# Rotary tables made in the first dilated pair, and HGRN2's level products held for both heads' updated queries

## The chip, the cores and the metric

The kernel runs on one core of a Trainium2 chip. A core has five engines that run side by side, each with its own queue of instructions in a fixed order: TensorE (PE, matrix products, results in PSUM banks), VectorE (DVE), ScalarE (ACT), GpSimd (POOL) and SyncE (SP), which here issues the DMA transfers. The metric is the device time of one execution in microseconds (us), the median of several runs. The time before is 1779.11 us, the median of three runs from 1778.2 to 1780.48.

## The reference

The function is a two-layer encoder on one sequence of 512 tokens with 1024 channels. Each layer makes one combined projection of its input and feeds three token mixers from it. Their outputs are gated, projected, merged, projected once more and normalized.

```python
def _layer(x, pos, ...):
    p = _split_in(jnp.einsum('bsd,dn->bsn', x, w_in) + b_in)
    y_a = _rms_norm(_hgrn2(p['hg_q'], p['hg_f_fwd'], p['hg_f_bwd'], p['hg_i'], lb_f, lb_b), hg_norm)
    y_a = y_a * jax.nn.silu(p['hg_g'])
    y_b = _dilated_mixer(groups) * jax.nn.silu(p['dil_g'])
    y_c = _mla(p['mla_cq'], p['mla_ckv'], p['mla_kr'], pos, g_q, g_kv, w_uq, w_ukv)
    y_c = y_c * jax.nn.silu(p['mla_g'])
    branch = jnp.einsum('nbsc,ncd->nbsd', jnp.stack([y_a, y_b, y_c]), w_branch)
    merged = jnp.sum(jax.nn.sigmoid(p['merge']) * branch, axis=0)
    return _layer_norm(ALPHA * x + jnp.einsum('bsd,de->bse', merged, w_out), ln_g, ln_b)
```

- A, HGRN2: a gated linear recurrence with eight heads, forward and backward in time: `S_t = diag(f_t) S_{t-1} + k_t v_t^T`, `o_t = S_t^T q_t`.
- B, dilated attention: eight heads in three groups of windows, with a linear bias by distance, a softmax in each group and a weighted sum over the groups.
- C, latent attention (MLA) with four heads. Part of its queries and keys is turned by a rotary embedding:

```python
ang = pos[..., None] * inv            # inv = theta ** (-i / half)
cos, sin = jnp.cos(ang), jnp.sin(ang)
x1 * cos - x2 * sin,  x2 * cos + x1 * sin
```

## The kernel before, in words

Activations lie with channels on the 128 partitions and the 512 tokens along the free dimension; a projection of 128 channels is one PSUM bank of 128x512. Every large product is made in three passes, since each operand is split into a high and a low part: high by high, low by high, high by low. With 1024 input channels that makes 24 matmuls of 128x512 per bank (`mm3`, L300; `tm` does the same with tokens on the partitions, L317). Weights come in chunks of 128x1024: SP loads a chunk into one of two raw buffers (L280), ACT copies the high part (L274), and POOL subtracts it from the raw chunk for the low part (L275; DVE for the chunks of HGRN2).

PSUM has four banks for projections, three for smaller products (`at_bank`) and one for outputs. Tiles in SBUF come from rotating pools by tag: `a2` has 16 buffers, `acc` 8, `f2` 8, `a4` 4, `f4` 6. A tile that takes a buffer waits for the last reader of the one before.

**The order.** The code is written as a sequence of calls, but a scheduler fixes the order on each engine when the kernel is built. It plans with its own estimates of how long each instruction takes, from the dependencies, the buffers and the order in the code. An edit that moves a call, or that adds a dependency, so changes the order of other work too. `after(first, *before)` adds such a dependency by hand: the instruction `first` waits for all of `before`.

**HGRN2.** The heads are worked on in four pairs. `hgrn_gates` makes for a head the query tile and the gate tiles `fr` (forget) and `kk` (keys) from three projections (hq, and hf twice). `in_tm(C_HI, "hv")` makes the values, whose banks DVE empties (L514). `hgrn_levels` is a generator that builds a head's 64-token block products by doubling the distance m = 1, 2, 4 ... 64. At each level the query tile `qq` and the key tile `kk` are multiplied in place by products of gates (L771 and L772, on DVE), so that the level's products (L754, on PE, tile `hs`) see the decayed queries and keys; ACT copies the keys into `kc` (L742) first. The products of level 4 are a case of their own (L723); the products of the higher levels are handed to the caller with `yield [made], products`, where `made` is the copy into `kc`. The caller runs the two heads of a pair in step, issues both heads' products one behind the other, and ties the first of them to both heads' `made`. Between these small groups PE runs the projections of the next pair. `hgrn_out` normalizes the outputs: a sum of squares (hgms, L534), the inverse root by small DVE instructions on 128x4 (hgrs), its spread over the partitions by a product (hgrb, L544), then the multiplications on DVE (L857, L858) and the split (L252).

**Dilated attention.** For each of four head pairs `dil_scores` makes the scores in four groups of small matmuls, two for the first window group (dsa, L924) and two for the others (dsb, L948). DVE adds the bias and takes the row minimum of the negated scores in the same instruction (`biased_min`, L895; tiles za and zb, minima in dst). The minima of both kinds go through DRAM to the other layout (L971 to L983) and come back as dso; DVE joins them (L990), ACT makes the exponentials (L996 for za, L1001 for zb), and later PE multiplies them with the values. Behind the first pair's exponentials in the code stands `merge(0, 0, ya)`, which begins the branch projection: PE's br products on the weights wb_0.

**Rotary tables.** `rope_tables` (L322) makes cos and sin of position times frequency once, in layer 0. It loads the positions (L327), reduces the angle to -pi..pi in exact steps by 43 DVE instructions on 128x512 (L329 to L378), and ACT takes two Sines (L376, L379) and makes four copies or scalings (L380 to L382). They are first read in `mla_rope`, behind all dilated pairs (at 642 us in the trace of before).

## Time and profile before

| | |
|---|---|
| median of three runs | 1779.11 us |
| profiled execution, its own time | 1780.54 us |
| its span | 1778.8 us |
| mean granted TensorE clock | 0.995 |
| busy: PE, DVE, ACT, POOL | 1745.7, 1048.8, 731.7, 574.6 us |

The span is the time from the first to the last instruction that the profiler saw; the profiled execution's own time lies 1.74 us above it. In a row of the timeline stand the start and the length in us, the engine, the line, the operation, output <- inputs with their kind, the count, and in brackets the idle time ahead of it with what ended it. Rows of the waits give the total, the number and the longest in us. Rows of groups give the busy time in us and the mean of one instruction in ns, and rows of windows give each engine's busy time in the order PE, weight loads, DVE, ACT, POOL, then the granted clock, the DMA share and GB/s.

### The profile page before, as it was taken

The numbers are of one execution on the slowest core, as the hardware profiler recorded it, in microseconds if no ns is written. First come the engines' busy times: TensorE is split into PE (matmuls) and PEld (weight loads), VectorE is DVE, ScalarE is ACT, GpSimd is POOL, SyncE is SP. The second block draws the span as 40 slices with busy tenths as digits, with TensorE's granted clock in tenths as the row PEclk, the third lists the DMA queues.
The fourth block names the chain that finished last, engine by engine and source line by source line (L and its number), as shares of the span: only waits on it lengthen the run. The fifth ranks groups of instructions, "written<-read, shape, count | busy, mean of one in ns | idle before, by whom it ended". The sixth has DMA issues, their size and how long they took to land.

```text
span 1778.8 us, 26441 instructions
## 1 busy us (share of the span) xinstructions
PE 1745.7 (98%) x10616; PEld 1451.2 (82%) x10616; DVE 1048.8 (59%) x1886; ACT 731.7 (41%) x1273; POOL 574.6 (32%) x338
## 2 busy tenths in 40 slices
PE   9999999999999999999999999999999999999987
PEld 7778978988888888887788888888888888888876
DVE  8888777443232566656577778775333225656566
ACT  6445453242424354433254355442424244434330
POOL 0412244233333243333213122532434332333341
PEclk9999999999999999999999999999999999999999
DMA  5223222223323222422242222222323222324222
GB/s 193 83 66 102 75 73 85 79 65 95 84 72 91 62 79 74 144 81 70 95 137 89 85 78 73 88 82 74 78 66 106 72 84 46 98 74 149 76 71 71
DMA packets 77146, 154.15 MB, mean 87 GB/s; under 512 B 37728, under 2 KB 37856, under 8 KB 77024
## 3 DMA queue, kind: packets, MB, share of 16 engines
q1 hardware_dynamic: 77024, 152.47, 28.0%
q8 instruction: 83, 1.36, 0.3%
q14 instruction: 39, 0.32, 0.1%
HBM read 148.15 MB, written 4.29 MB: 86 GB/s over the span
## 4 chain that ended last, share of the span: by engine, by line
PE 61%; DVE 4%; ACT 2%; DMA 1%; issue 1%; POOL 1%; SPq 0%; DVEq 0%; ACTq 0%
PE mg L300 14%; PE dl L300 6%; PE br L300 5%; PE wo L1236 5%; PE hf L300 4%; PE dv L317 4%; PE cq L300 2%; PE hq L300 2%; PE mo L659 2%; PE ckv L300 1%; PE hgg L300 1%; PE hv L317 1%; PE do L1016 1%; PE st L498 1%; PE qn L300 1%; PE dg L300 1%
## 5 line engine op out<-in xcount | busy, mean ns | idle before, releaser
L772 DVE TENSOR_TENSOR kk<-kk,fr 128x512 f32<-128x512 f32 x96 | 93.4, 992 | 32.8 <-ACT kc L742 21.7
L693 POOL TENSOR_TENSOR qq<-hq,fr 128x1024 f32<-128x1024 f32 x16 | 42.5, 2655 | 199.3 <-DVE fr L686 179.5
L771 DVE TENSOR_TENSOR qq<-qq,fr 128x512 f32<-128x512 f32 x96 | 75.3, 797 | 17.0 <-POOL qq L693 15.2
L1076 DVE TENSOR_SCALAR mg<-mg 128x512 f32<-128x512 f32 x32 | 53.4, 1680 | 54.0 <-ACT mg L1075 53.9
L895 DVE CUSTOM_DVE_ANT_0 zb<-dsb,con 128x256 f32<-128x256 f32 x64 | 23.3, 421 | 46.4 <-PE dsb L948 46.3
L764 DVE COPY_PREDICATED ha<-mask,hs 64x256 f32<-64x256 uint8 (+1 forms) x80 | 40.4, 505 | 16.7 <-PE hs L754 15.5
L655 ACT COPY mpt<-mtr 128x128 f32<-128x128 f32 x64 | 17.1, 266 | 77.7 <-DVE mpt L655 77.7
L275 POOL TENSOR_TENSOR wb_1l<-wb_1r,wb_1h 128x1024 fp32r<-128x1024 f32 x12 | 29.4, 2449 | 58.9 <-ACT wb_1h L274 45.0
L275 POOL TENSOR_TENSOR wb_0l<-wb_0r,wb_0h 128x1024 fp32r<-128x1024 f32 x12 | 29.4, 2448 | 58.8 <-ACT wb_0h L274 44.9
L878 DVE TENSOR_SCALAR dl<-dl,par,con 128x512 f32<-128x512 f32 x24 | 25.8, 1076 | 38.0 <-PE dl L300 37.9
L754 PEld LDWEIGHTS hs<-qq,kc 128*64 128x64 f32 x1024 | 33.3, 137 | 17.6 <-issue 8.8
L732 POOL TENSOR_SCALAR_AFFINE_SELECT ha<-hc 128x256 f32<-128x256 f32 x32 | 12.8, 424 | 105.0 <-ACT hc L727 104.8
L754 PE MATMUL hs<-qq,kc 128*64 128x64 f32 x1024 | 38.2, 225 | 5.6 <-DVE qq L771 5.6
L996 ACT ACTIVATE za<-za,dst 128x256 f32<-128x256 f32 x64 | 30.0, 471 | 33.4 <-DVE dst L990 33.4
L655 DVE COPY mpt<-mtr 128x128 f32<-128x128 f32 x64 | 18.5, 289 | 39.6 <-PE mtr L653 31.6
L713 POOL TENSOR_TENSOR hk<-kk,f 128x256 f32<-128x256 f32 x32 | 23.8, 745 | 51.5 <-DVE fr L775 51.5
L789 ACT COPY hkt<-hkt 128x384 f32<-128x384 f32 x32 | 15.4, 480 | 60.3 <-PE hkt L787 59.9
L1076 DVE TENSOR_SCALAR mgc<-mgc 128x512 f32<-128x512 f32 x16 | 24.8, 1547 | 25.0 <-ACT mgc L1075 25.0
L742 ACT COPY kc<-kk 128x512 f32<-128x512 f32 x64 | 37.6, 621 | 4.2 <-DVE kk L772 4.1
L650 DVE TENSOR_SCALAR mp<-mp,mst 128x512 f32<-128x512 f32 x32 | 35.6, 1112 | 0.9
L1201 DVE SCALAR_TENSOR_TENSOR res<-res,wo 128x256 f32<-128x256 f32 x32 | 12.1, 416 | 38.1 <-PE wo L1236 38.0
L659 PE MATMUL mo<-mpt,mv 128*128 128x128 f32 (+1 forms) x192 | 33.5, 309 | 0.0
(1509 smaller groups left out, 5408.5 us busy)
## 6 DMA issues: line engine op xcount, KB each, us to landing
wb_0r<-in_blocks_dram SPq DMA_DIRECT2D x12, 512.0 KB, 3.6
wb_1r<-in_blocks_dram SPq DMA_DIRECT2D x12, 512.0 KB, 3.6
w_0r<-in_blocks_dram SPq DMA_DIRECT2D x9, 512.0 KB, 3.6
w_1r<-in_blocks_dram SPq DMA_DIRECT2D x8, 512.0 KB, 3.6
w_2r<-in_blocks_dram SPq DMA_DIRECT2D x8, 512.0 KB, 3.5
w_3r<-in_blocks_dram SPq DMA_DIRECT2D x8, 512.0 KB, 3.6
wo_0r<-in_blocks_dram SPq DMA_DIRECT2D x8, 512.0 KB, 3.5
wo_1r<-in_blocks_dram SPq DMA_DIRECT2D x8, 512.0 KB, 3.5
```

Of the source, the lines that this page charges most:

```text
L275: (eng or nc.gpsimd).tensor_tensor(lo, raw, hi.bitcast(F32), ALU.subtract)
L300: newest["product"] = nc.tensor.matmul(ps, lhs(a, k), rhs(b, k), start=n == 0, stop=n == 3 * kt - 1)
L317: nc.tensor.matmul(ps, xs[a][2 * j + k][:, toks], w[b][:, k], start=j == 0 and n == 0, stop=j == 3 and n == 5)
L659: nc.tensor.matmul(o[:, cols], v[:, kb, h * 128:h * 128 + 128], pts[kb][:, cols], start=qt == 1 and kb == 0, stop=qt == NT - 1 and kb == N ...
L693: nc.gpsimd.tensor_tensor(qq, bcast(q, [[0, 2], [1, S]]), fr, ALU.mult)
L742: made = A.copy(fap(kc, 0, [[2 * m, R // 2], [m, 2], [1, m]]), fap(kk, 0, [[2 * m, R // 2], [S + m, 2], [1, m]]))
L754: mat = nc.tensor.matmul(sc[rows, to], kc[:, at], rhs, start=True, stop=True)
L764: ready = [V.copy_predicated(fap(a[rows], cols.start, [[128, NT], [1, wd]]), bcast(mk, [[0, NT], [1, wd]]), fap(sc[rows], cols.start, [[12 ...
L771: V.tensor_tensor(fap(qq, 0, dims), fap(qq, 0, dims), qf, ALU.mult)
L772: V.tensor_tensor(fap(kk, 0, dims), fap(kk, 0, dims), kf, ALU.mult)
L1076: V.tensor_scalar(g, g, 0.5, 0.5, ALU.mult, ALU.add)
L1236: nc.tensor.matmul(ps, ms[a][2 * kp + k][:, tt * 128:tt * 128 + 128], wo[4 * half + kp][b][k][:, cols], start=(kp, a, b, k) == (0, 0, 0, 0 ...
```

## The change

Two edits. The first moves `rope_tables()` from behind the values of HGRN2, at the start of layer 0, to behind the exponentials of the first dilated pair in layer 0, and lets its eight temporary tiles take buffers of the pool `acc` in place of `a2`. The second lets `hgrn_levels` hand out its last query update `turned` beside `made`, so that the first product of a level group waits for the query updates of both heads. No arithmetic is added or removed; one ACT table load falls away (7 to 6).

```diff
-        pos_i = t2("pos_i", I32)
+        pos_i = t2("pos_i", I32, "acc")
-        ang, n_, r, u, w = t2("r_ang"), t2("r_n"), t2("r_r"), t2("r_u"), t2("r_w")
+        ang, n_, r, u, w = [t2(f"r_{i}", tag="acc") for i in "anruw"]
...
-            t = t2(f"r_t{e}")
+            t = t2(f"r_t{e}", tag="acc")
...
-                    yield [made], products
+                    yield [made, turned], products
...
-                V.tensor_tensor(fap(qq, 0, dims), fap(qq, 0, dims), qf, ALU.mult)
+                turned = V.tensor_tensor(fap(qq, 0, dims), fap(qq, 0, dims), qf, ALU.mult)
...
         hv = in_tm(C_HI, "hv")
-        if l == 0:
-            shared["rope"] = rope_tables()
-        cosT, sinT, krT = shared["rope"]
...
             exps = dil_exp(hp, scores, behind)
+            if hp == 0:
+                if l == 0:
+                    shared["rope"] = rope_tables()
+                cosT, sinT, krT = shared["rope"]
```

How the order moves, at three places. First PE in the third head pair of layer 0, where `hs_16` and `hs_32` are the level products of two heads (query tiles 1889 and 1892 before, 1829 and 1832 now) and hq, hf and hgg are projections; before:

```order
L300 MATMUL hq_2314<-xh,w_896l 128x512 x2
L754 MATMUL hs_16_0_2023<-qq_0_1889,kc_16_0_2024 64x64 x8
L754 MATMUL hs_16_0_2026<-qq_0_1892,kc_16_0_2027 64x64 x8
L300 MATMUL hq_2314<-xh,w_896l 128x512 x6
L300 MATMUL hf_2350<-xh,w_1920h 128x512 x8
L300 MATMUL hf_2350<-xl,w_1920h 128x512 x8
L300 MATMUL hf_2350<-xh,w_1920l 128x512 x3
L754 MATMUL hs_32_0_2055<-qq_0_1889,kc_32_0_2056 64x64 x8
L754 MATMUL hs_32_0_2058<-qq_0_1892,kc_32_0_2059 64x64 x8
```

and the same place now:

```order
L300 MATMUL hq_2254<-xh,w_896l 128x512 x8
L754 MATMUL hs_16_0_1963<-qq_0_1829,kc_16_0_1964 64x64 x8
L754 MATMUL hs_16_0_1966<-qq_0_1832,kc_16_0_1967 64x64 x8
L300 MATMUL hf_2290<-xh,w_1920h 128x512 x8
L300 MATMUL hf_2290<-xl,w_1920h 128x512 x8
L300 MATMUL hf_2290<-xh,w_1920l 128x512 x8
L300 MATMUL hf_2325<-xh,w_2944h 128x512 x7
L754 MATMUL hs_32_0_1995<-qq_0_1829,kc_32_0_1996 64x64 x8
L754 MATMUL hs_32_0_1998<-qq_0_1832,kc_32_0_1999 64x64 x8
```

The group of level 16 stands six matmuls later, and 31 instead of 25 large matmuls (25 with the two pieces of hq and hf, 6 + 8 + 8 + 3) stand between it and that of level 32.

Second DVE at the first dilated pair of layer 0, now, from the first group of the dsb minima to the last one (`zb_0_3221` and `zb_0_3222` are the two heads' scores, the tiles named r belong to the rotary tables; before, one `dl` eviction, L878, stood between these two groups):

```order
L895 ISA zb_0_3222,dst_0_3217<-dsb_0_3252,con 128x256
L895 ISA dst_0_3217 128x1
L335 TENSOR_SCALAR r_w<-r_u 128x512
L336 TENSOR_SCALAR r_n<-r_n 128x512
L336 TENSOR_SCALAR r_w<-r_w 128x512
L371 SCALAR_TENSOR_TENSOR r_r<-r_n,r_r 128x512
L340 TENSOR_TENSOR r_u<-r_u,r_w 128x512
L878 TENSOR_SCALAR dl_0_3414<-dl_3421,par_161,con 128x128x4
L371 SCALAR_TENSOR_TENSOR r_r<-r_n,r_r 128x512 x2
L372 SCALAR_TENSOR_TENSOR r_r<-r_u,r_r 128x512
L895 ISA zb_0_3221,dst_0_3217<-dsb_0_3265,con 128x256
L895 ISA dst_0_3217 128x1
```

Eight rotary instructions stand here between two groups of minima; nine more stand ahead of the first dsb group, three ahead of the second dsa group and one within the last group. Seventeen stand ahead of L857, among the hgrs instructions.

Third ACT at the first dilated pair, now (w_10560h and wb_0h are high parts of weight chunks, `dl_0_3414` is the key half of the third window group):

```order
L274 CAST w_10432h<-w_10432r 128x1024
L274 CAST w_10560h<-w_10560r 128x1024
L376 ACT_TABLE_LOAD
L376 ACTIVATE sin<-r_r 128x512
L876 ACTIVATE dl_0_3414<-dl_3453,par_161 128x128x4
L381 ACTIVATE krt<-sin 32x512
L382 COPY krt<-sin 32x512
L379 ACTIVATE cos<-r_u 128x512
L380 COPY krt<-cos 64x512
L996 ACT_TABLE_LOAD
L996 ACTIVATE za_0_3219,dden_0_3515<-za_0_3219,dst_0_3217 128x256 x3
L996 ACTIVATE za_0_3219,dden_0_3515<-za_0_3219,dst_0_3217 128x128
```

Before, the table load of the exponentials followed w_10432h at once, and w_10560h, wb_0h, a gate activation and w_4352h followed the last exponential in this order; now wb_0h and w_4352h follow it, and the gate activation stands among the exponentials. On PE, 172 large matmuls stand between hgrb and the first br product where 214 stood: the projections of the dilated pair have moved ahead of hgrb, and behind the first br product of each of its two banks fifteen matmuls of the next `dl` projection are put in.

## The prediction

> **What bounds the kernel now.** I read the page's first part, then TensorE's waits, then the timeline of the places where the change works.
>
> ```profile
> PE 1745.7 (98%) x10616; PEld 1451.2 (82%) x10616; DVE 1048.8 (59%) x1886; ACT 731.7 (41%) x1273; POOL 574.6 (32%) x338
> ```
>
> ```profile
> PE hs L754 <- DVE qq L771: 5.6, 7, 1.0
> PE hq L300 <- DVE hv L514: 3.2, 1, 3.2
> ```
>
> TensorE (PE) sets the time, so an edit counts only by what PE waits for afterwards. The change touches both of these rows: the level products (L754) wait seven times, 5.6 us in all, for the query update of VectorE (DVE, L771), and one gate projection waits 3.2 us for a PSUM bank that DVE has yet to empty (L514). All in all only 33 us of the span are not PE's, and what the change does can be as large as any one of its waits. The timeline of PE shows these waits in the first head pair of layer 0, where DVE also makes the rotary tables, and the same stretch of layer 1, where no tables are made:
>
> ```profile
> 40.06 0.62 PE L317 MATMUL hv<-w_0h,xh 128*128 128x512 f32 x2
> ...
> 66.22 2.64 PE L300 MATMUL hq<-xh,w_256h 128*128 128x512 f32 x8 [3.16 <-DVE hv L514]
> 68.66 3.06 PE L300 MATMUL hq<-xl,w_256h 128*128 128x512 f32 x8
> 71.56 1.98 PE L300 MATMUL hq<-xh,w_256l 128*128 128x512 f32 x8
> ...
> 94.30 0.69 PE L754 MATMUL hs<-qq,kc 128*64 128x64 f32 x16 [0.77 <-DVE qq L771]
> ...
> 102.94 0.69 PE L754 MATMUL hs<-qq,kc 128*64 128x64 f32 x16 [0.66 <-DVE qq L771]
> 104.57 0.69 PE L754 MATMUL hs<-qq,kc 128*64 128x64 f32 x16 [0.95 <-DVE qq L771]
> ...
> 137.18 1.10 PE L723 MATMUL hs<-hq,hk 128*64 128x64 f32 x32
> ...
> 927.84 0.62 PE L317 MATMUL hv<-w_0h,xh 128*128 128x512 f32 x2
> ...
> 1017.29 1.10 PE L723 MATMUL hs<-hq,hk 128*64 128x64 f32 x32
> ```
>
> ```profile
> 50.00:75.00 25.00, 21.84 (x117) 17.69 (x116) 23.76 (x39) 7.34 (x11) 13.35 (x12) 0.93 0.27 85
> ```
>
> The last row is the stretch from 50 to 75 us: DVE (third value) is busy for 23.76 of 25 us and PE's granted clock, third from the end, is 0.93. The clock is low because of the wait: the sixteen matmuls behind it take 5.34 us (66.22 to 71.56); at the usual pace, 8 matmuls in 1.82 us or 0.2275 each, they take 3.64.
>
> **Term 1: the tables leave the first pair.** From the first product of hv to the second pair's first products layer 0 takes 97.12 us and layer 1 takes 89.45. The 7.67 us between them are the bank wait (3.16), the slow matmuls behind it (1.7), three level waits (2.38) and 0.4 of small gaps. With the tables gone nothing else distinguishes the two stretches, so I take **-7.65**. It needs nothing of the second edit, and the largest part, wait and clock, ends as soon as DVE empties hv's banks 3.2 us earlier; about half of the tables' work, estimated below, is enough for that.
>
> **Term 2: the hold on the level products.** The edit adds a dependency to the first product of a level: the query updates of both heads instead of none but those that the matmuls read. No work is added. The first head's products are held with the second's, so filler matmuls stand in front of the whole group where half of it used to run.
>
> ```profile
> 230.08 1.15 PE L754 MATMUL hs<-qq,kc 128*64 128x64 f32 x32
> ...
> 238.73 0.69 PE L754 MATMUL hs<-qq,kc 128*64 128x64 f32 x16 [0.96 <-DVE qq L771]
> ...
> 300.26 0.69 PE L754 MATMUL hs<-qq,kc 128*64 128x64 f32 x16 [0.59 <-DVE qq L771]
> ```
>
> Outside the first pair of layer 0 four waits are left: these two (third and fourth pair), and 5.6 - 2.38 - 0.96 - 0.59 = 1.67 for their two in layer 1. In the fourth pair the changed order puts 28 matmuls (6.4 us) ahead of the waiting group, where 22 stood (5.0); 1.4 us more is enough to cover both of its waits, 0.59 and about 0.7: **-1.3**. In the third pair 31 stand there instead of 25: 7.05 us, while the second head's update was done about 7.4 us after the group before (231.2 to 238.6). A wait of 0.3 remains in the good case, but a hold of DVE as in term 3, which costs some 2.0 us, would make it 2.3 for the whole group. Bounds for that pair in both layers together: -1.9 to +2.7. I take 0, near the middle. What queues behind a held group on PE are gate projections, which have spare DVE and ACT time; they are not priced.
>
> **Term 3: the tables in their new place.** 43 DVE instructions move; two of their rows give the prices of the two kinds:
>
> ```profile
> L340 DVE TENSOR_TENSOR r_t<-r_t,r_w 128x512 f32<-128x512 f32 x4 | 2.7, 685 | 0.0
> L336 DVE TENSOR_SCALAR r_w<-r_w 128x512 f32<-128x512 f32 x5 | 2.1, 418 | 0.0
> ```
>
> 25 with one input at 0.42 and 18 with two at 0.69 are 22.9 us. Now they stand in DVE's queue around the first dilated pair. Seventeen (8.8 us) lie ahead of the multiplication by the RMS factor (L857), among the small instructions that make the factor, in a stretch where DVE is mostly idle. From there to the last score minimum lie three (1.25 us), nine (5.1), eight (4.7) and one (0.4): 11.5 us in four places, each ahead of a pair of minima (L895). The rest follow the last minimum. What has these minima behind it is seen in PE's timeline, and in those of DVE, GpSimd (POOL), ScalarE (ACT) and the DMA queue:
>
> ```profile
> 351.15 1.05 PE L544 MATMUL hgrb<-con,hgrs0y 128*128 128x128 f32 x8
> ...
> 353.20 1.66 PE L300 MATMUL dl<-xh,w_4224h 128*128 128x512 f32 x6
> ...
> 373.44 1.16 PE L948 MATMUL dsb<-dl 64*128 64x128 f32 x16
> 374.53 0.50 PE L300 MATMUL dl<-xh,w_6272h 128*128 128x512 f32 x1
> ...
> 405.72 0.39 PE L300 MATMUL br<-ya00h,wb_0h 128*128 128x512 f32 x1
> ```
>
> ```profile
> 352.24 2.72 DVE L857 SCALAR_TENSOR_TENSOR hoc<-hoc,par,hgrb 128x512 f32<-128x512 f32 x4 [3.34 <-PE hgrb L544]
> ...
> 358.67 2.89 DVE L252 TENSOR_TENSOR ya00l<-hoc,ya00h 128x512 fp32r<-128x512 f32 x1
> ...
> 365.77 2.47 DVE L524 SCALAR_TENSOR_TENSOR dg0s<-dg0s,dg0z 128x512 f32<-128x512 f32 x1
> ...
> 371.96 1.22 DVE L878 TENSOR_SCALAR dl<-dl,par,con 128x512 f32<-128x512 f32 x1 [2.17 <-PE dl L300]
> 374.63 0.42 DVE L895 CUSTOM_DVE_ANT_0 zb<-dsb,con 128x256 f32<-128x256 f32 x1 [1.45 <-PE dsb L948]
> ...
> 376.01 0.08 DVE L895 DVE_READ_ACCUMULATOR2_ANT dst<- 128x1 f32 x1
> ...
> 385.42 1.33 DVE L990 TENSOR_TENSOR dst<-dst,dso 128x8 f32<-128x8 f32 x2
> ```
>
> ```profile
> 358.62 2.39 POOL L275 TENSOR_TENSOR w_6272l<-w_6272r,w_6272h 128x1024 fp32r<-128x1024 f32 x1 [5.25 <-PE dl L300]
> 365.30 2.39 POOL L275 TENSOR_TENSOR w_7296l<-w_7296r,w_7296h 128x1024 fp32r<-128x1024 f32 x1 [4.29 <-PE dl L300]
> ```
>
> ```profile
> 386.71 0.51 ACT L996 ACTIVATE za<-za,dst 128x256 f32<-128x256 f32 x1 [1.97 <-DVE dst L990]
> ...
> 393.91 1.15 ACT L876 ACTIVATE dl<-dl,par 128x512 f32<-128x512 f32 x1
> ...
> 395.23 0.19 ACT L1001 ACTIVATION_READ_ACCUMULATOR zb<-zb,dst 128x1 f32 x1
> ...
> 396.26 1.05 ACT L274 CAST wb_0h<-wb_0r 128x1024 fp32r<-128x1024 f32 x1
> ```
>
> ```profile
> 453.90 0.38 SPq L971 DMA_DIRECT2D db<-dst  x1
> ```
>
> ```profile
> 461.56 0.27 DVE L990 TENSOR_TENSOR dst<-dst,dso 128x8 f32<-128x8 f32 x2 [7.69 <-DMA dso<-db]
> ```
>
> The chain: minima, a round trip of the row minima through DRAM, the exponentials on ACT, and behind them on ACT's queue the cast of wb_0h, which the first branch product (L300, br) needs. I time it from hgrb's start, 351.15.
>
> - Last minimum, before: 376.09, so 24.9. DVE was idle for 2.17 + 1.45 = 3.6 in it, which the moved work fills. 24.9 + 11.5 + 0.4 (a dl eviction of 1.2 moves in, one of 0.8 moves out) - 3.6 = 33.2.
> - Holds: two of the rows above take 2.89 and 2.47 us instead of about 0.68. Each starts just after a weight split began on POOL and ends with it, so a hold costs about 2.0. Two of the four splits between 351 and 375 held DVE in this way. A split comes per 24 matmuls (5.46 us): about six in 33 us, and the share of DVE's work that goes from SBUF to SBUF rises. I take two more holds, +4.0: 37.2. Bounds: none more, and four more (+8.0).
> - Round trip, 453.90 to 461.56 where DVE is free: 7.7, and 0.3 for the issue: 8.0.
> - From L990 to the first exponential 1.3 (385.42 to 386.71).
> - Exponentials from 386.71 to 395.42, less 1.0 for L876, which now lies ahead: 7.7; a gate activation now among them 0.7; the cast 1.05.
>
> Sum 55.9 us after hgrb. PE gets to br with fewer matmuls between: 172 instead of 214, 39.1 us, and the small groups, 2.05 for hgrb and the first dsa (351.15 to 353.20), about 1.0 for the second, 1.09 for each dsb: 5.2. So PE is there at 44.3, where it used to be at 54.6 with the cast done at 397.31, 8.4 us early. PE waits **+11.6** between hgrb and br, at the dsb groups and at br together; bounds +7.6 and +15.6.
>
> [...]
>
> **Small terms.** Behind wb_0h comes the cast for the next dl chunk, 1.05, and only two br matmuls (0.45) stand before the matmul that needs it: **+0.6**. A wait of some 6 us at br is longer than the 3.16 that cost 1.7 of slow clock: **+1.5**, bounds 0 (the wait is cut up) and 1.7. At no cost: both Sine activations, their table load and the copies, hidden in the round trip of 8.0 (without that cover they would add their five to six us, estimated from the 1.2 us that L876 takes and six such steps, to the exponentials); the position DMA, which is issued well before DVE's cast of it; the eight tiles that change their tag, as the accumulators of that pool are first used behind br.
>
> **Sum:** -7.65 - 1.3 + 11.6 + 0.6 + 1.5 = +4.75. Against the profiled 1780.54 (1778.8 of span and 1.7 around it) that is 1785.3. The profiled execution lies 1.4 over the median of the three runs, so against 1779.11 it is 1783.9; I say **1784**. The rivals' times are against the median too.
>
> **Rivals.**
>
> *No change (about 1779).* The tables cause no further hold. Then 7.6 instead of 11.6 is waited, and with 1.0 for the clock the sum is +0.25: 1779.4. For it: in the same rows two of four splits held nothing. Against it: the denser queue.
>
> *Faster (about 1774).* One mechanism: POOL's splits are released by PE (its row: `<-PE dl L300`), and a PE that waits at the dsb groups shifts them to where DVE reads minima out of PSUM, which shows no stretching (0.42 at L895). If neither the two old holds nor new ones fall on DVE, 7.6 becomes 3.6, and the clock stays up: -7.65 - 1.3 + 3.6 + 0.6 = -4.75, 1774.4. It decides from a wait of 4.8 downward. Against it: 11.5 us of DVE work in a row of about 34 can hardly dodge six splits of 2.4.
>
> *Heavier (about 1791).* Every split that starts in these 33 us holds DVE, where two of four did before: 15.6, the third pair's +2.7, 1.7 for the clock: -7.65 - 1.3 + 2.7 + 15.6 + 0.6 + 1.7 = +11.65, 1790.8. [...]
>
> *The hold doesn't do what it says.* It is a dependency, and PE may still stop in front of a level group for as long as before; then -1.3 is lost: +6.05, 1785.2.
>
> **How the numbers follow.** Chances: forecast 0.54, no change 0.27, faster 0.08, heavier 0.06, hold without effect 0.05. The forecast's own range goes from one hold more and no slow clock (+1.25, 1780.4) to three more, 1.7 for the clock and half of the third pair's +2.7 (+8.3, 1787.4). To hold 8 in 10 the range has to take in most of the no-change case: 1776.5 to 1789.5. A measurement of this kernel can tell about 0.2% (3.6 us) from no change: below 1775.6 is faster, above 1782.7 slower. Of the forecast about seven tenths, 0.39, lie above 1782.7, with the heavier case and the hold without effect 0.50; the rest of the forecast and the no-change case, 0.42, lie within; 0.08 below.
>
> **What would show it.** Term 1: no wait of hq for hv, clock 1.00 from 50 to 75 us, and 89 to 90 us from hv to the second pair. Term 2: L754's waits fall to two or so, in the third pair. Term 3: waits of PE at dsb for DVE's minima and one of about 6 us of br for the cast of wb_0h at L274, slow matmuls behind it, rope instructions of 2 us and more. I am wrong if br waits less than 3 us, or if the first pair of layer 0 keeps a wait that the tables did not cause.

## The result, and the profile after

The changed kernel takes 1791.39 us, the median of five runs (1788.32 to 1792.12), against 1780.4 for the kernel before (five runs, 1778.2 to 1782.11). The ratio is 1.0054, with a 95% interval from 1.0043 to 1.0066: slower by 11 us. The profiled execution took 1791.39 us as well, with a span of 1789.7 us and a granted clock of 0.994; its span is 10.9 us longer than that of before. The forecast had the sign and less than half of the size, and its range ends 1.9 us below the measured time.

TensorE's waits after, with the total, the number and the longest in us:

```profile
PE br L300 <- ACT wb_0h L274: 5.9, 2, 3.7
...
PE dsb L948 <- DVE dst L895: 4.0, 2, 2.2
PE hs L754 <- DVE qq L771: 3.2, 2, 1.6
...
PE br L300 <- POOL wb_0l L275: 1.9, 1, 1.9
```

The bank wait of hq for hv is gone, and the level waits (L754) are two instead of seven. In their place stand waits of br and of dsb, 11.8 us together (5.9, 4.0 and 1.9), and there are more of them than were forecast: br waits twice for wb_0h, and once for its low part. The row of windows from 50 to 75 us shows the first head pair without the tables, VectorE (third value) at 16.36 us instead of 23.76 and the granted clock at 1.00:

```profile
50.00:75.00 25.00, 25.00 (x164) 20.44 (x163) 16.36 (x24) 9.09 (x14) 5.33 (x10) 1.00 0.35 107
```

TensorE's timeline gives the ends of that pair, and then the first dilated pair of layer 0:

```profile
40.25 0.61 PE L317 MATMUL hv<-w_0h,xh 128*128 128x512 f32 x2
...
129.66 1.10 PE L723 MATMUL hs<-hq,hk 128*64 128x64 f32 x32
...
352.77 1.12 PE L544 MATMUL hgrb<-con,hgrs0y 128*128 128x128 f32 x8
...
371.81 1.16 PE L948 MATMUL dsb<-dl 64*128 64x128 f32 x16 [1.79 <-DVE dst L895]
...
381.06 2.08 PE L948 MATMUL dsb<-dl 64*128 64x128 f32 x16 [2.19 <-DVE dst L895]
...
407.31 0.73 PE L300 MATMUL br<-ya00h,wb_0h 128*128 128x512 f32 x2 [3.68 <-ACT wb_0h L274]
408.84 3.78 PE L300 MATMUL dl<-xh,w_4352h 128*128 128x512 f32 x8 [0.80 <-ACT mg L1075]
...
415.21 0.40 PE L300 MATMUL br<-ya00h,wb_0l 128*128 128x512 f32 x1
```

From hv to the second pair's first products it is 89.41 us (40.25 to 129.66), where it was 97.12. The first dilated pair waits four times, 8.46 us in all. Behind br the fifteen matmuls of `dl` take 6.4 us (408.84 to 415.21) where 15 at 0.2275 take 3.4: the clock is at half speed, granted 0.50 in each window of 1 us from 409 to 414. The next TensorE rows are from the second dilated pair, where nothing was forecast:

```profile
497.63 0.50 PE L300 MATMUL br<-ya00h,wb_0h 128*128 128x512 f32 x1 [2.20 <-ACT wb_0h L274]
500.06 0.63 PE L300 MATMUL br<-ya00h,wb_0l 128*128 128x512 f32 x1 [1.93 <-POOL wb_0l L275]
...
507.00 1.25 PE L1027 MATMUL dta<-con,za 128*128 128x128 f32 x10
```

The account, in us, along points that both traces have. The first transposes of the exponentials (dta, L1027) end a dilated pair here; up to those of the first pair the changed order does fifteen `dl` matmuls more (3.4 us). They are subtracted in that row and added in the next, where they are missing.

| stretch of the span | measured, after less before | forecast |
|---|---|---|
| start to hv | +0.2 | 0 |
| first head pair | -7.7 | -7.65 |
| from there to dta of the first dilated pair (411.16 before, 420.21 after) | +13.2 | +13.7, less 0.65 of term 2 |
| second dilated pair, dta to dta (to 495.06 before, 507.00 after) | +6.3 | 0 |
| all that follows, layer 1 with it | -1.1 | -0.65 |
| sum | +10.9 | +4.75 |

The miss is nearly all in one row: the second dilated pair.

What happened there stands in SP's queue, which issues the transfers. The row sums of the exponentials (dden) go through DRAM to the other layout as the minima do: two writes into the buffer dd (L981), two reads back (L982, L983). The timeline of SP's queue after, then the DMA view of the stretch from 473 to 492 us:

```profile
473.38 0.37 SPq L981 DMA_DIRECT2D dd<-dden  x1
473.85 0.45 SPq L280 DMA_DIRECT2D w_11072r<-in_blocks_dram  x1
475.25 0.36 SPq L981 DMA_DIRECT2D dd<-dden  x1
491.94 0.33 SPq L982 DMA_DIRECT2D dso<-dd  x1
...
492.88 0.36 SPq L280 DMA_DIRECT2D wb_0r<-in_blocks_dram  x1
```

```profile
DMA packets 1201, 0.54 MB, mean 29 GB/s; under 512 B 1072, under 2 KB 1072, under 8 KB 1200
...
w_11072r<-in_blocks_dram SPq DMA_DIRECT2D x1, 512.0 KB, 12.4
```

And the same queue before:

```profile
463.76 2.23 SPq L981 DMA_DIRECT2D dd<-dden  x2
474.37 0.33 SPq L982 DMA_DIRECT2D dso<-dd  x1
...
475.29 0.37 SPq L280 DMA_DIRECT2D w_11072r<-in_blocks_dram  x1
476.13 0.36 SPq L280 DMA_DIRECT2D wb_0r<-in_blocks_dram  x1
```

Before, the two writes go out together and SP can read back 8.4 us after the end of the second (463.76 + 2.23 to 474.37); the loads of w_11072 and wb_0 follow the reads. After, the load of w_11072 stands between the two writes. 1072 of the 1201 packets of that stretch are under 512 bytes, all 0.54 MB move at a mean of 29 GB/s, the load of 512 KB takes 12.4 us, and the read back comes 16.3 us after the end of the second write (475.25 + 0.36 to 491.94). Everything behind it in SP's queue is late, and that is wb_0, whose cast and low part br waits for.

### The profile page after: what moved, and what is told of

It reads as the page before. It is cut to its first block, busy times and chain, and to the rows that moved or that the text cites. A ratio compares the mean times of both kernels' runs of the same rounds, so it can differ in the third digit from the quotient of the medians.

```text
span 1789.7 us, 26422 instructions
## 1 busy us (share of the span) xinstructions
PE 1748.2 (98%) x10616; PEld 1452.6 (81%) x10616; DVE 1060.6 (59%) x1886; ACT 730.0 (41%) x1272; POOL 572.1 (32%) x338
## 4 chain that ended last, share of the span: by engine, by line
PE 85%; DVE 8%; DMA 3%; ACT 2%; issue 1%; POOL 1%; SPq 0%; DVEq 0%; ACTq 0%; POOLq 0%
PE mg L300 14%; PE dl L300 12%; PE hf L300 8%; PE dv L317 8%; PE br L300 6%; PE wo L1237 4%; PE hq L300 4%; PE hgg L300 2%; PE hv L317 2%; PE cq L300 2%; PE hs L754 2%; PE do L1016 2%; PE mo L659 2%; PE dg L300 2%; PE st L498 1%; PE ckv L300 1%
## 5 line engine op out<-in xcount | busy, mean ns | idle before, releaser
L771 DVE TENSOR_TENSOR qq<-qq,fr 128x512 f32<-128x512 f32 x96 | 82.5, 872 | 24.6 <-POOL qq L693 15.0
L754 PEld LDWEIGHTS hs<-qq,kc 128*64 128x64 f32 x1024 | 32.5, 138 | 14.2 <-issue 10.1
L996 ACT ACTIVATE za<-za,dst 128x256 f32<-128x256 f32 x64 | 30.0, 470 | 30.2 <-DVE dst L990 30.2
L878 DVE TENSOR_SCALAR dl<-dl,par,con 128x512 f32<-128x512 f32 x24 | 25.8, 1074 | 27.2 <-PE dl L300 27.2
L754 PE MATMUL hs<-qq,kc 128*64 128x64 f32 x1024 | 36.9, 225 | 3.2 <-DVE qq L771 3.2
L742 ACT COPY kc<-kk 128x512 f32<-128x512 f32 x64 | 37.2, 619 | 5.5 <-DVE kk L772 5.5
```

The lines of the kernel that those rows point to most:

```text
L742: made = A.copy(fap(kc, 0, [[2 * m, R // 2], [m, 2], [1, m]]), fap(kk, 0, [[2 * m, R // 2], [S + m, 2], [1, m]]))
L754: mat = nc.tensor.matmul(sc[rows, to], kc[:, at], rhs, start=True, stop=True)
L771: turned = V.tensor_tensor(fap(qq, 0, dims), fap(qq, 0, dims), qf, ALU.mult)
```

## The experiments

Line numbers in the rows of an experiment move by up to seven where its edit adds lines. The time before is the median of the runs that the experiments of one chip share: 1781.32 us for the two edits apart, the load between the writes and the first kernel with the tables behind the third pair; 1781.16 for GpSimd's splits and the three kernels with the positions loaded early; 1780.83 for the four with narrow tables.

### The two edits apart

The tables moved, without the hold:

```diff
-                    yield [made, turned], products
+                    yield [made], products
```

> The tables move as in the change, and the level products aren't held (the second edit undone). In the order of this kernel the two DRAM writes of the second dilated pair's sums (L981, dd) stand one behind the other again; in the changed kernel the load of w_11072 stands between them. Theory (queue): the 6.3 us that the changed kernel loses between the first and the second pair's transposes (a wait of 2.2 for wb_0h, one of 1.9 for wb_0l, slow clock 2.2) come from that place in the DMA queue. Then they are gone: 7.7 gained in the first head pair, 13 lost in the first dilated pair, about 0.7 of the fourth pair's level waits back in each layer, 1785 to 1787 beside 1780.4. Rival (late chain): the second pair's branch weights are late because everything in the first dilated pair is late; then the two waits stay, at about 1791.

Measured: 1783.44 us, ratio 1.0010 [1.0000, 1.0019], 2.1 us over the kernel before. Its first pair takes 89.45 us, so the gain of term 1 is there in full. The second dilated pair takes 83.9 us, as before: its waits of br are gone, as the queue theory says, though the whole is faster than its 1785 to 1787. Of its waits, two belong to the new place:

```profile
PE dsb L948 <- DVE dst L895: 3.0, 1, 3.0
PE mg L300 <- ACT w_10560h L274: 2.6, 1, 2.6
```

The hold, with the tables in their old place:

```diff
-                    yield [made], products
+                    yield [made, turned], products
...
-                V.tensor_tensor(fap(qq, 0, dims), fap(qq, 0, dims), qf, ALU.mult)
+                turned = V.tensor_tensor(fap(qq, 0, dims), fap(qq, 0, dims), qf, ALU.mult)
```

> The tables stay where they were and the level products are held for both heads' queries. Theory: the hold alone moves little. The bank wait of 3.2 us with its slow clock in layer 0's first head pair stays; level waits fall or grow by a microsecond here and there: -2 to +2 against before, 1778.5 to 1782.5. Rival (the hold is what costs): the groups that it pushes back make a wait of their own, over 1784, and the change without it would be no slower than before.

Measured: 1781.82 us, ratio 1.0002 [0.9991, 1.0014].

```profile
PE hs L754 <- DVE qq L771: 2.9, 3, 1.6
```

The level waits fall from 5.6 to 2.9 us, and the time doesn't move by more than its interval of about 2 us to each side. The expectation holds. In the first pair a bank wait of 3.1 us stays, with a granted clock of 0.62 from 64 to 73 us behind it, and that pair takes 96.1 us, 1.1 less than before.

The two edits don't add. Apart they cost 2.1 and 0.5 us, together 11.0; 8.4 us exist only when both are there. What they share can be read from the orders: between hgrb and the first br product of layer 0 stand 214 large matmuls before, 194 with the hold alone, 194 with the tables alone, and 172 with both. Each edit by itself takes 20 matmuls, 4.6 us at 0.2275, from the cover of the chain that ends in wb_0h. That chain was 8.4 us early in the kernel before: it can lose this once, and not twice, above all when the tables lengthen it. The traces bear this out: with the tables alone the cast of wb_0h ends 52.9 us after hgrb, 6.3 us before TensorE comes to br, and five splits of GpSimd hold VectorE there too; with both edits it ends at 54.5 us, with 22 large matmuls (5.0 us) fewer beside it, and br waits. And with neither edit alone does a weight load stand between the two writes of dd. In the profiled executions 5.2 us of what the edits cost only together lie between hv and dta of the first dilated pair (less the fifteen `dl` matmuls, as in the account), and 6.3 in the second pair; the rest of the span differs by up to 3.6 us between these four executions and takes some of it back. The part of the second pair is tested in the next experiment; that the cover makes the other part is read from the orders and traces, and no run changes it alone.

### The load between the two writes

The changed kernel, with one dependency more: the load of w_11072 in layer 0 is put behind the second write of dd. In the order that results it stands behind the two reads as well; TensorE, VectorE, ACT and GpSimd do the same instructions in the same order as in the changed kernel.

```diff
+        if name == "w0_11072":
+            after(load, newest["stored"])
...
-                nc.sync.dma_start(buf[i, 64:576].rearrange("(j p) -> p j", p=128), src[:, 0, i])
+                last = nc.sync.dma_start(buf[i, 64:576].rearrange("(j p) -> p j", p=128), src[:, 0, i])
+            newest["stored"] = last
```

> The changed kernel with one dependency more: in layer 0 the load of w_11072 waits for the second dd write of the second dilated pair. Nothing else is asked for, though the order may move with it. Theory (queue): dd lands in about 8 us instead of 16, the load in 4 instead of 12, wb_0 comes in time, and the second pair's branch products wait for nothing: 4.1 of waits and about 2 of slow clock less, 1785 to 1786. Rival (late chain): the load was late anyway, and the waits of 2.2 and 1.9 stay within a microsecond: 1790 to 1792.

Measured: 1788.28 us, ratio 1.0041 [1.0026, 1.0056]: 7.0 us over the kernel before instead of 11.0, and more than the 1785 to 1786 of the theory. The intervals of the two kernels overlap, so the comparison rests on the traces. SP's waits from 460 to 490 us, and TensorE's timeline:

```profile
SPq L985 <- DMA dd<-dden: 8.9, 1, 8.9
```

```profile
405.10 1.22 PE L302 MATMUL br<-ya00h,wb_0h 128*128 128x512 f32 x2 [4.61 <-ACT wb_0h L274]
...
487.70 2.14 PE L302 MATMUL mg<-xh,w_11072h 128*128 128x512 f32 x8 [1.34 <-ACT mg L1078]
```

The wait for the writes is 8.9 us again, the load takes 4 us, and both br waits of the second dilated pair are gone. From dta to dta that pair takes 82.17 us instead of 86.79, 4.6 us less. So the place of one transfer in SP's queue is worth most of the unforeseen 6.3 us; of the rest, 1.34 is the wait in the last row. The first dilated pair still waits.

### GpSimd's splits under the tables

The changed kernel, with the low parts of five weight chunks made by ACT as a copy and no longer by GpSimd (the subtraction is left out):

```diff
-        (eng or nc.gpsimd).tensor_tensor(lo, raw, hi.bitcast(F32), ALU.subtract)
+        if name in ("w0_5760", "w0_6272", "w0_7296", "w0_7808", "w0_8832"):
+            A.copy(lo, raw)
+        else:
+            (eng or nc.gpsimd).tensor_tensor(lo, raw, hi.bitcast(F32), ALU.subtract)
```

> The changed kernel; for the five weight chunks that GpSimd splits while the first dilated pair of layer 0 runs (w_5760, w_6272, w_7296, w_7808, w_8832) the low part is replaced by a second copy of the raw chunk, made on ScalarE (1.05 us each): the subtraction is left out, so the output isn't the reference's. GpSimd then stands still there. In the changed kernel the last score minimum ends 38.0 us after the start of hgrb, with five DVE instructions of 1.9 to 2.9 us in between whose usual length is 0.4 to 0.7: 10 us more than they need. Theory (the shared hold): without GpSimd's splits these five take their usual length, and the last minimum comes 28 to 29 us after hgrb, or as soon as PE gets there; the dsb waits vanish. Rival (they are long for another reason, such as the writes of ScalarE or DMA to the same tiles): instructions of 2 us and more stay, and the last minimum stays at 36 to 38.

In the changed kernel the rows that this is about are those of VectorE and of GpSimd between hgrb and the last score minimum:

```profile
356.57 2.59 DVE L858 TENSOR_TENSOR hoc<-hoc,hgg0s 128x512 f32<-128x512 f32 x1
363.47 2.90 DVE L252 TENSOR_TENSOR ya20l<-hoc,ya20h 128x512 fp32r<-128x512 f32 x1
369.27 1.94 DVE L335 TENSOR_SCALAR r_w<-r_t 128x512 f32<-128x512 f32 x1
377.11 2.77 DVE L363 TENSOR_TENSOR r_u<-r_u,r_t 128x512 f32<-128x512 f32 x1
387.49 2.63 DVE L335 TENSOR_SCALAR r_n<-r_r 128x512 f32<-128x512 f32 x1
```

```profile
356.22 2.39 POOL L275 TENSOR_TENSOR w_7296l<-w_7296r,w_7296h 128x1024 fp32r<-128x1024 f32 x1 [5.22 <-PE dl L300]
...
387.45 2.39 POOL L275 TENSOR_TENSOR w_10560l<-w_10560r,w_10560h 128x1024 fp32r<-128x1024 f32 x1 [8.11 <-PE dl L300]
```

Five splits start in that stretch, and each has a held VectorE instruction that ends 0.3 or 0.55 us behind it (356.22 + 2.39 = 358.61, and 356.57 + 2.59 = 359.16): first the split, then the instruction. Less their own 0.42 or 0.68, the five last 10.0 us too long, 2.0 each. The edit takes three of these five splits from GpSimd (w_7296, w_7808 and w_8832). From VectorE's and TensorE's timelines of that kernel:

```profile
374.50 2.87 DVE L343 TENSOR_TENSOR r_u<-r_u,r_w 128x512 f32<-128x512 f32 x1
```

```profile
351.96 1.05 PE L547 MATMUL hgrb<-con,hgrs0y 128*128 128x128 f32 x8
...
369.07 1.16 PE L951 MATMUL dsb<-dl 64*128 64x128 f32 x16
...
376.05 1.16 PE L951 MATMUL dsb<-dl 64*128 64x128 f32 x16
```

Measured, in one execution: 1786.96 us, so without an interval. Up to the last minimum one held instruction is left, beside the split of w_10432, which the edit leaves on GpSimd; the one beside the split of w_10560 now follows the last minimum. Both waits of dsb are gone, as the theory says, and the last minimum ends 30.2 us after hgrb instead of 38.0 (the theory had 28 to 29): 7.8 us for four holds less. That the tables' new place pays for GpSimd's splits is shown, with the price; the order of the other instructions is that of the changed kernel. A wait of 3.0 us of br for wb_0h remains. The waits of the second dilated pair are there as in the changed kernel, with the load of w_11072 between the two writes and 15.9 us from the end of the second to the read.

### The tables behind another pair

The third dilated pair in place of the first, with the old tags and with the hold:

```diff
-            if hp == 0:
+            if hp == 2:
```

> The changed kernel, but the tables are called for behind the exponentials of the third dilated pair instead of the first, with their old a2 buffers (all eight acc buffers are in use there). In its order all 43 rotary instructions stand between two pairs' minima, none ahead of a minimum that a transfer waits for in the same pair. Theory: the 7.7 of the first head pair are kept, and where DVE has room between the pairs the tables cost nothing: no wait at dsb, none of br for wb_0h in the first or the second pair; 7.7 less than before, 1772 to 1774. Rival (the tables cost their price in any dilated pair): waits of 5 us and more in the third or fourth pair, 1779 or more.

Measured: 1788.49 us, ratio 1.0042 [1.0027, 1.0058]. The first two dilated pairs are as quick as the new first head pair allows: the second ends at 487.8, 7.3 us before that of the kernel before. The third gives it back in one wait, as the rival says. From VectorE's timeline and from TensorE's:

```profile
556.72 0.43 DVE L329 CAST r_a<-pos_i 128x512 f32<-128x512 int32 x1 [9.88 <-DMA pos_i<-in_positions_dram]
```

```profile
575.73 1.97 PE L1027 MATMUL dtb<-con,zb 128*128 128x128 f32 x8 [12.05 <-DVE dta20p L1032]
```

VectorE idles for 9.88 us in front of the tables, since the load of the positions is issued behind the reads of dd, at 551.9 us. So the positions were loaded at the start of the kernel, into the tile that later holds the cosines, and the tables tried in two places and without the hold:

```diff
-        pos_i = t2("pos_i", I32, "acc")
-        nc.sync.dma_start(pos_i, bass.AP(positions.tensor, positions.offset, [[0, 128], [1, S]]))
+        pos_i = cos.bitcast(I32)
...
+            shared["cos"] = cst.tile([128, S], F32, name="cos")
+            nc.sync.dma_start(shared["cos"].bitcast(I32), bass.AP(positions.tensor, positions.offset, [[0, 128], [1, S]]))
```

> The kernel rope_hp2 with the positions loaded at the start of the program into the tile that later takes cos, so that the cast needs no transfer at that place. In rope_hp2 DVE stood still for 9.9 us until the positions came (their DMA was queued behind a read that waits for the dd writes), 21 rotary instructions lay ahead of the copy of the third pair's transposes (L1032), and PE waited 12.0 us for it. Theory: the late positions are the cause. The tables start 10 us earlier, the wait falls from 12.0 to 2 or 3, and with the slow clock behind it less the kernel is at 1774 to 1778, faster than before by 4 to 7. Rival (the 21 instructions themselves, with holds, are too long for that place): a wait of 7 us or more stays, 1781 to 1786.

> e_rope_hp2 without the second edit. Theory (the hold does nothing by itself): within 2 us of e_rope_hp2. Rival (the hold spoils the order wherever the tables are): faster than e_rope_hp2 by 3 us and more.

> The positions loaded at the start, the tables behind the exponentials of the second dilated pair (acc buffers), the level products not held. In the order, most rotary instructions lie among the copies of the first pair's transposes, and eight ahead of minima of the second pair. Theory (it matters who waits for DVE there): 7.7 gained in the first head pair, small waits of the transposes and at the dsa and dsb groups, 1774 to 1780. Rival (any place in a dilated pair costs about 9, as in rope_only): 1782 and more.

Measured: behind the third pair 1783.09 us with the hold (1.0009 [0.9999, 1.0019]) and 1782.98 without it (1.0015 [1.0006, 1.0024]); behind the second pair without the hold 1784.88 (1.0020 [1.0011, 1.0029]). From the first of the three, TensorE's timeline:

```profile
571.20 1.97 PE L1026 MATMUL dtb<-con,zb 128*128 128x128 f32 x8 [7.93 <-DVE dta20p L1031]
```

Five rotary instructions are held there too (2.50 to 2.83 us), ahead of the copy of the transposes that TensorE waits for, and the 7.7 us won in the first head pair go in a wait of 7.93 (7.2 without the hold). So in both places it is the rival that came out. Behind the second pair the row minima and wb_0h are late instead, by 1.93 and 4.05 us. The hold makes no difference behind the third pair, as its theory says: 1783.09 and 1782.98.

### Less VectorE work for the tables

Frequencies fill only 32 partitions, and the 128 partitions hold them four times. So the tables can be computed once, in quarter width: each quarter of the tokens on 32 partitions of a 128x128 tile. Sixteen copies on ACT (sine) and sixteen on VectorE (cosine) then spread them.

```diff
+        pos_i = t2("pos_i", I32)[:, :128]
+        for q in range(4):
+            nc.sync.dma_start(pos_i[32 * q:32 * q + 32],
+                              bass.AP(positions.tensor, positions.offset + 128 * q, [[0, 32], [1, 128]]))
+        ang, n_, r, u, w, sq, cq = [t2(f"r_{i}")[:, :128] for i in "anruwsc"]
...
+        for q in range(4):
+            rows, cols = slice(32 * q, 32 * q + 32), slice(128 * q, 128 * q + 128)
+            for c in range(4):
+                A.copy(sin[32 * c:32 * c + 32, cols], sq[rows])
+                V.tensor_copy(cos[32 * c:32 * c + 32, cols], cq[rows])
```

It was run in the old place and in the new one, each with the hold and without it.

> The kernel before with the tables made in a quarter of the width, at their old place: the four copies of the 32 frequencies on the partitions each take another quarter of the tokens, so that the 43 instructions work on 128x128, and 16 copies of 32x128 each on ScalarE and VectorE spread sin and cos afterwards. Level products not held. DVE's work on the tables falls from 22.9 us to an estimated 8 to 12 (no row here shows these shapes; a 128x128 minimum takes 0.28). Theory (DVE's time on the tables makes the waits of the first head pair): bank wait and slow clock vanish and the level waits shrink; 5 to 7.7 faster than before, ratio 0.9957 to 0.9972. Rival (the place or the order, not the time): the bank wait of about 3 stays, ratio 0.999 to 1.001.

> c_old with the second edit, the hold on the level products. Theory (the hold does nothing by itself): the same as c_old within 2 us. Rival (it spoils other stages' order once the first pair is quick): 3 us and more slower than c_old.

> The changed kernel, its place and its hold, with the tables in a quarter of the width. Theory (what the new place costs is DVE's time ahead of the minima, stretched by holds): with 8 to 12 us instead of 22.9, some 5 instead of 11.5 of it between hgrb and the last minimum, PE's waits at dsb and br fall from 8.5 to 0 to 4, 1774 to 1781. Rival (the order that goes with the new place costs, whatever the tables take): the waits of br in the first and second pair stay above 5 us together, 1785 and more.

> c_after without the hold, to be read beside rope_only (1783.4 with the tables at full width). Theory: waits at dsb and br of 0 to 2 us instead of 5.6, 1773 to 1777. Rival: within 2 us of rope_only.

| tables in quarter width | median, us | ratio, 95% interval |
|---|---|---|
| old place | 1778.55 | 0.9985 [0.9977, 0.9994] |
| old place, hold | 1778.63 | 0.9985 [0.9976, 0.9994] |
| new place | 1779.83 | 0.9995 [0.9986, 1.0004] |
| new place, hold | 1788.08 | 1.0041 [1.0026, 1.0056] |

The two kernels with the old place are the quickest of the study, 2.3 us faster than the kernel before (the theory had 5 to 7.7): less than the 3.6 us that the prediction took for what can be told, though both intervals exclude no change. Groups of VectorE from the first of them:

```profile
L386 DVE COPY cos<-r_c 32x128 f32<-32x128 f32 x16 | 3.5, 218 | 0.2
L342 DVE TENSOR_TENSOR r_t<-r_t,r_w 128x128 f32<-128x128 f32 x4 | 1.2, 290 | 0.1
```

An instruction at quarter width takes 0.22 or 0.29 us instead of 0.42 or 0.69, the tables with their copies 14.2 us instead of the 22.9 that the prediction worked out. The first pair takes 93.5 us, 3.6 less than before. A wait is left that takes the place of the bank wait: 2.3 us of hv for the low part of w_3, which VectorE makes behind the tables. The hold does nothing there, as expected. In the new place without the hold the time lies between the theory (1773 to 1777) and the rival.

In the new place the hold costs 8.25 us with narrow tables too (1788.08 and 1779.83), and 0.1 in the old one. SP's queue with the hold, at the first dilated pair:

```profile
394.39 0.37 SPq L988 DMA_DIRECT2D dd<-dden  x1
394.85 0.45 SPq L280 DMA_DIRECT2D w_4352r<-in_blocks_dram  x1
396.25 0.36 SPq L988 DMA_DIRECT2D dd<-dden  x1
412.69 0.33 SPq L989 DMA_DIRECT2D dso<-dd  x1
```

TensorE's timeline of the same kernel:

```profile
423.00 0.90 PE L1034 MATMUL dta<-con,za 128*128 128x128 f32 x3 [4.30 <-DVE dta00p L1039]
```

And SP's queue without the hold:

```profile
390.12 2.24 SPq L988 DMA_DIRECT2D dd<-dden  x2
401.48 0.33 SPq L989 DMA_DIRECT2D dso<-dd  x1
```

The same event in another pair and with another weight: a load between the two writes (12.2 us to its landing), and 16.1 us from the end of the second write to the read (396.61 to 412.69) where 9.1 pass without it (from the end of the row of two, 392.36, to 401.48). Of the fourteen kernels, three have a load at such a place: the changed one, the one with five splits less, and this one. All three have hold and tables in the new place together, and in all three the read comes 15.9 to 16.3 us after the end of the second write; in all other pairs of dd writes it is 7.7 to 9.1. The wait of 4.30 us can be followed back to the late read: the copy dta00p stands on VectorE behind a merge gate (L1083) that waits for ACT, ACT waits 8.63 us for w_4864, and SP loads w_4864 behind the reads, at 413.62. Behind that wait the granted clock is 0.62 from 419 to 428 us. So the time is that of the rival, 1785 and more, but not by its waits: br waits only 2.8 us. Here, too, the cover shrinks, from 209 to 187 large matmuls between hgrb and br. How the whole of the 8.25 us splits between load and cover, no run of this pair separates.

## Why the prediction was right or wrong

**Term 1, the tables leave the first pair: right.** 7.71 us measured, 7.65 forecast; the bank wait, the level waits of that pair and the low clock went together. The same stretch of the other layer was the right ruler. The kernels with the tables elsewhere have it too: 89.45 us with the tables moved alone, 89.40 with them behind the third pair.

**Term 2, the hold: the waits fell, the gain can't be seen.** The two waits that the forecast expected are there, 1.61 us each, in the third pair of each layer. Outside the first pair the level waits were 3.21 us before and are 3.22 after: the fourth pair wins 0.6 to 0.7 per layer and the third loses 0.65. The -1.3 rested on taking 0 for the third pair. With the hold alone the interval reaches from -1.6 to +2.5 us, which doesn't exclude -1.3. This is the rival of a hold without effect, in its size but not in its way. That the hold does something quite different, to the order of other work, was not in the term.

**Term 3 with the small terms: right in sum, by two errors that cancel.** 13.2 us measured in that stretch, 13.7 forecast. The last minimum ends 38.0 us after hgrb (forecast 37.2): there were five held instructions and not four, and 1 us less of the rest. The round trip of the minima took 6.1 us and not 8.0, as SP issued the read 1.95 us after the write (390.83 to 392.78) where the pair that gave the price has 3.67 (453.90 to 457.57); why it could, no run shows. br starts 54.5 us after hgrb, forecast 55.9. The waits on this way are 7.66 us up to br (1.79, 2.19 and 3.68) and 0.80 for the `dl` chunk behind it (forecast 11.6 and 0.6). What the waits lack, the clock has: the forecast put 1.5 us at one spot, and there were 3.4 us of half speed at dsb (between 380 and 385) and 6.8 behind br (between 408 and 415). They cost 1.6 and 3.2 us. The window behind br:

```profile
407.00:416.00 9.00, 7.89 (x21) 5.93 (x22) 3.67 (x2) 2.66 (x5) 4.87 (x2) 0.62 0.37 110
```

A granted clock of 0.62 over 9 us is 6.8 us at half speed. So the near agreement of this sum is luck in its parts. On ACT, the step from L990 to the first exponential took 1.1 us (396.89 to 397.97; forecast 1.3), but not for L990 alone: the table load of the exponentials (1.28 us from 396.67), which the prediction doesn't name, ends 0.5 us behind the second join (397.28 + 0.17). The five to six us that the prediction gives for the hidden ACT work don't follow from six steps of 1.2 us, which make 7.2; one table load, two Sines and three copies (not four) took 4.4.

**The step that failed: "Small terms", which stops at the first br product.** It prices what stands behind wb_0h up to the next dl chunk, and nothing after that. The step should have followed SP's queue on: the orders, which were there to be read, show a load between the two writes of dd in the second dilated pair, and wb_0 behind their reads. What the step puts at nothing cost 6.3 us: waits of 2.20 and 1.93, 1.7 of slow clock behind them, and small gaps. With the load behind the reads, and no other engine's order changed, 4.6 of the 6.3 us went. With that row, the sum would have been +11. The prediction's signs of being wrong look at the first head pair and at the first br alone, so neither shows this. What the order could not have told is the size, as no trace of before has a load between these writes.

**The rivals.** The heavier case, 1790.8, came within 0.6 us of the measured time, by chance. Its mechanism held in part: all five splits of the stretch held VectorE. But its price didn't: its wait up to br was to be 15.6 us and was 7.7, since the splits were five, the round trip was shorter and the slow clock took a part; the rest of the measured time came from the second dilated pair, of which it says nothing. The faster case had no part in it: TensorE did wait at dsb, and the splits still fell on the tables. Nor had the rival of no change, which needed that no further hold came.

**What was missing in the frame.** The prediction adds one term for each edit. The runs show that the edits aren't separate: 8.4 of the 11 us come from their meeting. One way is the order of SP's queue, which a run shows; the other, as far as the traces tell, is the cover (twice 20 matmuls).

## What to carry to other kernels

Where a scheduler sets the order, price an edit by the order that results, on every engine and on the DMA queue, to the end of the phase and not only to the first wait; an edit that costs nothing alone may use up the slack that the next one needs. Work that is moved under another engine's long instructions is paid at the price of its holds, here 2.0 us for each split of GpSimd, so making it smaller gained 2.3 us where moving it to three other places gained nothing. And keep a large load from standing between two small scattered writes that someone waits for: here the load took 12.4 us to land instead of about 4.

## What the runs showed of the hardware

- **A load between two scattered writes was slow, and so were they.** 512 KB took 12.4 and 12.2 us to land, against about 4 us behind the writes, and the time from the end of the second write to the read back grew from 8 or 9 us to 16. It was seen at two pairs with two weights, and putting the load behind the writes and their reads removed it at the one where it was tried. Why the two slow each other was not measured.
- **The clock fell after some waits of about 2 us and not after others, so the length of the wait alone doesn't decide.** Half speed followed waits of 2.19 us (dsb at 381.06; the granted clock is 0.82 from 381 to 390 us) and 2.20 (br at 497.63; 0.81 from 497 to 506), and none followed 1.79 us at 371.81 (1.00 from 370 to 379). But the changed kernel with the one load moved waits the same 1.79 us at the same place, and there half speed follows:

```profile
370.76 1.16 PE L950 MATMUL dsb<-dl 64*128 64x128 f32 x16 [1.79 <-DVE dst L897]
```

```profile
370.00:379.00 9.00, 8.24 (x40) 6.70 (x41) 8.76 (x28) 1.05 (x1) 1.47 (x1) 0.81 0.06 0
```

And a wait of 2.33 us in the kernel with narrow tables in the old place (hv at 60.60) leaves the clock at 1.00 from 50 to 75 us. What decides was not settled. In the slow time matmuls start 0.43 us apart instead of 0.23 (br from 500.06), and in windows of 1 us the granted clock is down to 0.50. While matmuls run, the traces of before and after have seven such stretches, six of 3.4 us and one of 6.8 (behind br, between 408 and 415), added up from those windows.
